# A decoder trunk on one core: head 0's gates and values take turns by two row tiles, with all first transfers on one queue in smaller parts, and one pair of heads' values a piece sooner

## The chip, the cores and the metric

The kernel runs on one core of one Trainium2 chip. The metric is the device time of one execution in microseconds (us), and the times given are medians over executions. TensorE (PE) does the matrix products, VectorE (DVE), ScalarE (ACT) and GpSimd (POOL) the elementwise work, and transfers are started from the queues of SyncE (SP), ACT and POOL.

## The reference

The input `x` is 256 rows of 2048 float32 values. Two layers are computed, each followed by a squared-ReLU MLP. The first is RetNet retention with 8 heads, the second latent attention with 16 heads. What the change touches is the projection of retention and, in one place, the attention:

```python
h = rms_norm(x, norm_mix[0])
q, k, v, gate = split(h @ w_in)         # 8 heads: q, k of 256 columns, v and gate of 512 each
q, k = apply_rope(q), apply_rope(k) * 256 ** -0.5
scores = einsum('bhcnd,bhcmd->bhcnm', q, k) * decay
o = scores @ v  (+ the state of the earlier chunk)
x = x + (silu(gate) * rms(o)) @ w_out
...
p = softmax(q_nope @ k_nope + q_pe @ k_pe, causal)      # latent attention, 16 heads
x = x + (p @ v) @ w_o
```

The norms' factors are applied late: the kernel multiplies the bare `x` (times a gain per column) by the weights, and the row factor `r0` comes in when results are read out.

## The kernel before, in words

**Numbers in two parts.** Every float32 operand of a matrix product is split into a high part (a cast on ACT, `wh` for weights) and a low part (the rest, a subtraction on DVE, `wl`), both in `split`, lines 185 to 195. One product is then three matmuls: high by high, high by low, low by high. A low part is thus first needed one matmul after its high part.

**Weights in pieces.** All weights stream through in pieces of 128 x 2048 float32 values, 1 MB, started from SP's queue into four buffers `raw`. Each piece is split in two halves of 128 x 1024 (`wh` and `wl`, five buffers each). A piece of a plain product takes 24 matmuls of 512 columns. Later heads and the MLPs use a variant (`quad`, `gemm_pair`) in which DVE also forms sums of weight blocks (lines 339 to 343) and of activations (`with_sums`, lines 419 to 421), in exchange for fewer products.

**Order by hand.** `tick` counts pieces. `later(n, fn)` puts a step into a list, to be emitted `n` pieces later. The emitted order is the order within each engine, up to a scheduler that may let an instruction pass another one on the same engine. Eight semaphores serve the transfers started from SP and ACT in turn, so that each such transfer waits until the one eight before it has landed.

**PSUM.** There are four banks `acc` for products, two banks `tp` for transposes, scores and attention outputs, and a pair `at`.

**The beginning.** For head 0, `gemm(a["ret_w_gv0"], 0, ..., "rg0", gated, start)` computes the gates in four pieces, each of four row tiles of `x` by 512 columns, into two `acc` banks. Row tiles are the 128-row tiles of the 2048 input features, 16 in all. These four pieces are loaded in parts: 256 KB twice, then 512 KB. After the first part of each half `start(half)` loads two row tiles of the transposed input (`x0t`, 256 KB) and splits them (`first_inputs`). The constants (`pos_i`, `cst`, `gpe`) are loaded at half 3. The sine tables of rope begin at half 5 (`ret_tables`; DVE casts the positions, POOL does the rest). After the gates come `rq0` and `rk0` (queries and keys, two pieces each, `gemm_t`), and then four pieces `rv0` with the values, into two `acc` banks. The loads of `x` itself share the time with `rq0` and `rk0`: `load_x`, two pieces after the last half of the gates is begun and on, brings 8 tiles of 256 KB by SP, takes their sums of squares on ACT, and writes each tile to `x_home` in DRAM from POOL's queue.

**Head 0's results.** `gated` copies the gates out of PSUM on ACT as soon as the last gate piece is done, and `silu` follows eight pieces later when `r0` is known. Rope of q and k waits six and four pieces (`ret_rope`), the scores five (`ret_scores`), the products with the values one piece after the last value piece (`ret_out`). From `ret_out` of head 0 three things are timed: the transposes and splits of its output `y`, 2 pieces later, the angles `tm` of the attention's rope on POOL, and 25 pieces later `mla_tables`, which makes the table `petab` with 16 small DVE operations (lines 575 and 578).

**Heads 1 to 7** run as `rq`, `rk` and 8 pieces `rp` each: `rp1`, `rp2`, ... In the names of the trace `rp14_wl2` would be head 1, piece 4, split 2. The trace leaves the numbers out, so they go by time here.

**Attention.** Eight pairs of heads `b` go through `query`, `turn`, `score`, a second `turn` and `values`, spaced in pieces by a table:

```python
waits = [(3, 3, 3, 2)] * 6 + [(3, 3, 2, 2), (2, 2, 2, 1)]
```

`values(b)` computes `ao` in a `tp` bank (lines 1156 and 1157), and the split of `ao` (`ot`, ACT and DVE) frees the bank. Transposes of a later pair's queries (`qntp`, `qptp`) take turns in the same two banks. After the attention comes the output product `wo`.

Of the kernel before, what the change touches and what calls it, by code (L numbers as in the profile page):

```python
# [20 lines left out]
P = 128  # L21
# [47 lines left out]
def yoco(ctx: ExitStack, tc: tile.TileContext, a):  # L69
# [141 lines left out]
                nc.tensor.transpose(tp[:, j, t * P : (t + 1) * P], srcs(t, j), ident)  # L211
        return tp

    def stream(w, chunk, cols, name, use, done=None, before=None):

        raw = pool.tile([P, 2048], F32, tag="raw", bufs=4, name=f"{name}_raw")
        if before is None:
            nc.sync.dma_start(raw[:, :cols], w[chunk])
        n = cols // 2
        for half in range(2):  # L220
            wh = pool.tile([P, 1024], F32R, tag="wh", bufs=5, name=f"{name}_wh{half}")
            wl = pool.tile([P, 1024], F32R, tag="wl", bufs=5, name=f"{name}_wl{half}")
            cuts = 1
            if before is not None:
                cuts = 1 if half else 2
                m = n // cuts
                for i in range(cuts):
                    lo = half * n + i * m
                    nc.sync.dma_start(raw[:, lo : lo + m], w[chunk][:, lo : lo + m])
                    if i == 0:  # L230
                        before(half)
# [9 lines left out]
    def piece(w, chunk, acc, act, g, nk, nb, name, before=None, done=None):  # L241

        if before is None:
            need(act, 2 * g + 2)

        def use(half, wh, wl):
            for j in range(2):
                k = g * 4 + half * 2 + j
                rh, rl = (v[:, j * nb : (j + 1) * nb] for v in (wh, wl))
                for t in range(NT):  # L250
                    ah, al = (act[k // 2][:, j, i, t * P : (t + 1) * P] for i in range(2))
                    nc.tensor.matmul(acc[t], ah, rh, start=k == 0, stop=False)
                    nc.tensor.matmul(acc[t], ah, rl, start=False, stop=False)
                    nc.tensor.matmul(acc[t], al, rh, start=False, stop=k == nk - 1)

        stream(
            w, chunk, 4 * nb, f"{name}{g}", use, done and (lambda: done(acc)),
            before and (lambda half: before(2 * g + half)),
        )

    def gemm_t(w, chunk0, act, nk, name, done):

# [163 lines left out]
    def accs(nb, name):  # L426
        return [bank("acc", [nb], f"{name}_acc{t}") for t in range(NT)]

    def gemm(w, chunk0, act, nk, nb, name, done, before=None):

        acc = accs(nb, name)
        n = nk // 4
        for g in range(n - 1):
            piece(w, chunk0 + g, acc, act, g, nk, nb, name, before)
        last_piece(w, chunk0, acc, act, nk, nb, name, done, before)

    def last_piece(w, chunk0, acc, act, nk, nb, name, done, before=None):
        g = nk // 4 - 1
        piece(w, chunk0 + g, acc, act, g, nk, nb, name, before, done)

    def gemm_blocks(w, chunk_of, act, nk, name, done):

# [73 lines left out]
    def sincos(inv, w, name, pos_f=pos_f):  # L516

        n = NT * w

        def f2k(shape, name):  # L520
            return shaped(act_tile(name, F32).rearrange("p j i s -> p (j i s)"), shape)

        ang = f2k([NT, w], f"{name}_ang")
        for t in range(NT):
            nc.gpsimd.tensor_scalar(ang[:, t], inv, pos_f[:, t : t + 1], None, op0=ALU.mult)
        flat = ang.rearrange("p t w -> p (t w)")
        k = f2k([2, n], f"{name}_k")
# [24 lines left out]
        nc.gpsimd.tensor_scalar(r, r, lim, -lim, op0=ALU.min, op1=ALU.max)  # L552

        def finish(zero):
            sc = f2k([2, n], f"{name}_sc")
            nc.scalar.activation(sc, r, AF.Sin, bias=zero)
            return sc.rearrange("p i (t w) -> p i t w", t=NT)

        return finish
# [20 lines left out]
                    )  # L580

    def ret_tables():
        nc.vector.tensor_copy(pos_f, pos_i)
        ret_sc.append(sincos(cst[:, C_INVR : C_INVR + 128], 128, "tr"))

    def scale_tables():
# [12 lines left out]
        later(2, turn)  # L599


    act0, sums0, r0, ret_sc, mla_sc, no_turn = [], [], [], [], [], []

    def first_inputs(c):

        t = f2k([2, S], f"x0t_{c}")
        nc.sync.dma_start(t, a["xt"][:, 2 * c : 2 * c + 2, :])
        v = act_tile(f"a0_{c}")
        split_act(v, t, [gain(G_MIX0 + 2 * c + j) for j in range(2)])
        act0.append(v)  # L610
# [1 line left out]
        if c in HEAD:  # L612
# [19 lines left out]
    def load_x(b):  # L632
        for t in range(NT):
            x0 = f2k([512], f"x0_{t}{b}")
            nc.sync.dma_start(x0, x_in(t, b))
            square_sum(x0, ss0[t][:, b : b + 1], f"n0_{t}{b}")
            nc.gpsimd.dma_start(x_home[t][b], x0)

    def start(half):
        first_inputs(half)  # L640
        if half == 3:
            nc.sync.dma_start(pos_i, a["pos"])
            nc.sync.dma_start(cst, a["cst"])
            nc.sync.dma_start(gpe, a["gpe"])
        if half == 5:
            ret_tables()
        if half == 7:
            for b in range(NB):
                later(2 + b, lambda b=b: load_x(b))
            later(6, scale_tables)  # L650

    def ret_rope(acc, out, name, wait):

        u = f2k([2, S], f"{name}_u")
        for i in range(2):
            nc.scalar.copy(u[:, i], acc[i][:, S:])
            nc.vector.tensor_tensor(u[:, i], acc[i][:, 0:S], u[:, i], op=ALU.add)
# [81 lines left out]

    def ret_projected(h, qk, gate, v, s):  # L740

        wait = 0 if h else 8

        def keyed(acc):
            ret_rope(acc, qk, f"rk{h}", max(wait - 4, 0))
            later(max(wait - 4, 0) + (2 if h else 1), ret_scores(h, qk, s))

        gemm_t(a["ret_w_qk"], h * 2, act0, KD, f"rq{h}", lambda acc: ret_rope(acc, qk, f"rq{h}", max(wait - 2, 0)))
# [23 lines left out]
    for h in range(RH):  # L772
        qk, gate, v, s = [], [], [], []
        if h == 0:

            def gated(acc, gate=gate):
                src = [f2k([512], f"gate_raw{t}") for t in range(NT)]
                for t in range(NT):
                    nc.scalar.copy(src[t], acc[t])

                def silu():
                    for t in range(NT):
                        g = f2k([512], f"gate0{t}")
                        nc.scalar.activation(g, src[t], AF.Silu, scale=r0[t])
                        gate.append(g)

                later(8, silu)
# [3 lines left out]
            gemm(  # L791
                a["ret_w_gv0"], 4, act0, KD, 512, "rv0",
                lambda acc, v=v, s=s, gate=gate: ret_valued(acc, 0, s, v, gate),
            )
            continue

        def paired(c, h=h, gate=gate, v=v, s=s):
# [474 lines left out]
```

## Time and profile before

| what | value |
|---|---|
| time, median of 3 runs | 2460.23 us (2459.69 to 2460.62) |
| profiled execution, its time | 2459.91 us |
| profiled execution, span from first to last instruction | 2458.1 us |
| granted TensorE clock | 1.000 |
| PE busy | 2448.9 us, 11626 matmuls |
| DVE busy | 2199.1 us |
| ACT busy | 1617.8 us |
| POOL busy | 251.1 us |
| DMA | 522.10 MB, mean 212 GB/s |

The span leaves out 1.8 us of the profiled execution's time. PE's busy time is an upper view, because matmuls overlap and their ends are modelled. The gap between the starts of two matmuls in a row tells more: it is 0.227 us for 512 columns when PE waits for nothing. A row of a timeline gives the start, the duration of one instruction or a run of them, engine, line of the kernel, operation, output and inputs, form and count. The bracket at its end gives the idle time of that engine just before it and what ended it.

### The profile page before, as it was taken

How to read it: one execution, taken by the hardware profiler on the slowest of the kernel's cores; microseconds unless marked ns; L12 is line 12 of the kernel's file. 1: busy time of each engine (PE TensorE's matmuls, PEld its weight loads, DVE VectorE, ACT ScalarE, POOL GpSimd, SP SyncE). 2: the span in 40 equal slices, each digit the busy share in tenths (PEclk: the TensorE clock that was granted, in tenths of full speed). 3: DMA queues.
4: the chain of work that ended last, by engine and by line, in shares of the span. 5: the costliest groups of instructions: out<-in, count | busy, mean ns of one | idle time of the engine just before them, and what ended most of it. 6: DMA issues, size and time to landing. Idle time of an engine off the chain costs nothing.

```text
span 2458.1 us, 31782 instructions
## 1 busy us (share of the span) xinstructions
PE 2448.9 (100%) x11626; PEld 2057.3 (84%) x11626; DVE 2199.1 (89%) x2859; ACT 1617.8 (66%) x2280; POOL 251.1 (10%) x311
## 2 busy tenths in 40 slices
PE   9999999999999999999999999999999999999999
PEld 7888888888888888888888888998888888888887
DVE  7799999889899999999999998776689999999998
ACT  6566656566676667667666777676566666676665
POOL 7400011000010010110110001100000101101101
PEclk9999999999999999999999999999999999999999
DMA  9645568546564685674785564445645856857856
GB/s 324 218 174 208 194 204 248 193 178 218 204 237 180 207 261 215 209 257 173 245 268 206 184 222 182 160 147 195 201 176 197 260 211 209 270 198 226 261 188 188
DMA packets 93980, 522.10 MB, mean 212 GB/s; under 512 B 11136, under 2 KB 12288, under 8 KB 40576
## 3 DMA queue, kind: packets, MB, share of 16 engines
q1 hardware_dynamic: 70992, 471.25, 53.4%
q0 software_dynamic: 22400, 48.25, 9.1%
q8 instruction: 91, 1.49, 0.2%
q10 hardware_dynamic: 432, 0.57, 0.1%
q14 instruction: 65, 0.53, 0.1%
HBM read 479.14 MB, written 41.94 MB: 212 GB/s over the span
## 4 chain that ended last, share of the span: by engine, by line
PE 99%; ACT 1%; DVE 0%; DMA 0%; issue 0%; POOL 0%; SPq 0%; ACTq 0%; POOLq 0%
PE u_c L378 7%; PE u_c L376 7%; PE u_c L377 7%; PE d_c L377 7%; PE d_c L378 7%; PE d_c L376 7%; PE rp_c L377 3%; PE rp_c L378 3%; PE rp_c L376 3%; PE rk_acc L280 2%; PE rq_acc L280 2%; PE u_p L376 2%; PE u_p L378 2%; PE u_p L377 2%; PE d_p L376 2%; PE d_p L377 2%
## 5 line engine op out<-in xcount | busy, mean ns | idle before, releaser
L191 ACT CAST u_wh<-u_raw 128x1024 fp32r<-128x1024 f32 x362 | 347.8, 991 | 207.5 <-DVE u_raw L339 98.3
L191 ACT CAST d_wh<-d_raw 128x1024 fp32r<-128x1024 f32 x342 | 327.4, 989 | 185.5 <-DVE d_raw L339 93.9
L192 DVE TENSOR_TENSOR u_wl<-u_raw,u_wh 128x1024 fp32r<-128x1024 f32 x362 | 401.6, 1142 | 46.2 <-ACT u_wh L191 40.9
L192 DVE TENSOR_TENSOR d_wl<-d_raw,d_wh 128x1024 fp32r<-128x1024 f32 x342 | 378.2, 1140 | 30.8 <-ACT d_wh L191 26.2
L376 PE MATMUL u_c<-u_wh,n 128*128 128x512 f32 x706 | 276.5, 392 | 0.0
L377 PE MATMUL u_c<-u_wl,n 128*128 128x512 f32 x706 | 275.6, 390 | 0.0
L378 PE MATMUL u_c<-u_wh,n 128*128 128x512 f32 x706 | 275.0, 390 | 0.0
L376 PE MATMUL d_c<-d_wh,hid 128*128 128x512 f32 x654 | 256.0, 392 | 0.0
L377 PE MATMUL d_c<-d_wl,hid 128*128 128x512 f32 x654 | 255.4, 390 | 0.0
L378 PE MATMUL d_c<-d_wh,hid 128*128 128x512 f32 x654 | 254.8, 390 | 0.0
L191 ACT CAST rp_wh<-rp_raw 128x1024 fp32r<-128x1024 f32 (+1 forms) x166 | 158.8, 981 | 128.3 <-DVE rp_raw L339 65.2
L192 DVE TENSOR_TENSOR rp_wl<-rp_raw,rp_wh 128x1024 fp32r<-128x1024 f32 (+1 forms) x166 | 183.9, 1135 | 18.5 <-ACT rp_wh L191 16.5
L378 PEld LDWEIGHTS u_c<-u_wh,n 128*128 128x128 f32 x706 | 132.5, 188 | 27.4
L376 PEld LDWEIGHTS u_c<-u_wh,n 128*128 128x128 f32 x706 | 132.6, 188 | 27.1
L377 PEld LDWEIGHTS u_c<-u_wl,n 128*128 128x128 f32 x706 | 132.6, 188 | 26.6
L378 PEld LDWEIGHTS d_c<-d_wh,hid 128*128 128x128 f32 x654 | 122.8, 188 | 25.4
L376 PEld LDWEIGHTS d_c<-d_wh,hid 128*128 128x128 f32 x654 | 122.8, 188 | 25.1
L377 PEld LDWEIGHTS d_c<-d_wl,hid 128*128 128x128 f32 x654 | 122.8, 188 | 24.6
L156 POOL DMA_DIRECT2D xh<-d_c x52 | 45.1, 867 | 934.4 <-ACT d_c L396 932.5
L191 ACT CAST ro_wh<-ro_raw 128x1024 fp32r<-128x1024 f32 x88 | 85.6, 996 | 59.4 <-DVE ro_raw L339 25.2
L376 PE MATMUL rp_c<-rp_wh,a 128*128 128x512 f32 x286 | 111.8, 391 | 0.0
L377 PE MATMUL rp_c<-rp_wl,a 128*128 128x512 f32 x286 | 111.3, 389 | 0.0
(546 smaller groups left out, 6143.6 us busy)
## 6 DMA issues: line engine op xcount, KB each, us to landing
u_raw<-in_mlp_w SPq DMA_DIRECT2D x128, 1024.0 KB, 5.3
d_raw<-in_mlp_w SPq DMA_DIRECT2D x120, 1024.0 KB, 4.9
rp_raw<-in_ret_w_gv SPq DMA_DIRECT2D x56, 1024.0 KB, 4.9
ro_raw<-in_ret_w_out SPq DMA_DIRECT2D x32, 1024.0 KB, 5.0
uq_raw<-in_mla_w_uq SPq DMA_DIRECT2D x24, 768.0 KB, 4.1
rq_raw<-in_ret_w_qk SPq DMA_DIRECT2D x16, 1024.0 KB, 4.8
rk_raw<-in_ret_w_qk SPq DMA_DIRECT2D x16, 1024.0 KB, 5.1
wo_raw<-in_mla_w_o SPq DMA_DIRECT2D x16, 1024.0 KB, 4.8
```

Source lines behind the costliest of these rows:

```text
L156: nc.gpsimd.dma_start(x_home[t][2 * p + j], part, accum_op=ALU.add)
L191: nc.scalar.copy(h, src)
L192: nc.vector.tensor_tensor(l, src, h.bitcast(F32), op=ALU.subtract)
L280: nc.tensor.matmul(acc[f], wh[:, cols], a.rearrange("p i s -> p (i s)"), start=k == 0, stop=k == nk - 1)
L376: nc.tensor.matmul(dst, ah, bh, start=n == 0, stop=False)
L377: nc.tensor.matmul(dst, ah, bl, start=False, stop=False)
L378: nc.tensor.matmul(dst, al, bh, start=False, stop=n == total[key] - 1)
```

## The change

Head 0's gate and value columns are laid side by side in DRAM by two row tiles: 8 pieces `gv0` to `gv7`, each with 12 matmuls of the gates and then 12 of the values for the same two row tiles. All four `acc` banks are held through the 8 pieces, and `rq0` and `rk0` follow them. There are 12 pieces for head 0 as before.

All first transfers are on SP's queue in smaller parts: piece 0 as four parts of 256 KB with its `x0t` as two of 128 KB, placed between them, and each other piece as 512 KB, 256 KB of `x0t`, 512 KB. `cst` is loaded in two parts. The loads of `x` move into the new loop, ahead of `gv4` to `gv7`, and the writes to `x_home` are issued from ACT's queue in place of POOL's. The cast of the positions moves from DVE to POOL, and the rope tables start at piece 2.

When the last piece is done, `raws` copies gates and values out of PSUM (four copies on ACT). Every wait of head 0 is set anew: rope 3 and 1 pieces, scores 2, `silu` 5, the values' splits 4 and `ret_out` 4 more. `ret_out` of head 0 thus comes at tick 16, where it came at 13, and with it the transposes of its `y` and `mla_tables` come three pieces later than before. The sine on ACT gets a copy in front of it that ties it behind the first rope copy (`late`). The loads of `x0s` for the sums of activations are timed anew. In the attention table the pair `b = 4` gets a last wait of 1 in place of 2.

```diff
-    def stream(w, chunk, cols, name, use, done=None, before=None):
+    def stream(w, chunk, cols, name, use, done=None, load=None):
         raw = pool.tile([P, 2048], F32, tag="raw", bufs=4, name=f"{name}_raw")
-        if before is None:
+        if load is None:
             nc.sync.dma_start(raw[:, :cols], w[chunk])
+        else:
+            load(raw)
...
-            cuts = 1
-            if before is not None:
-                cuts = 1 if half else 2
...
+            cuts = 2 if load and chunk == 0 else 1
...
+    def rows_256(acc, v, wh, wl, nb, first, last):
+        for j in range(2):
+            rh, rl = (w[:, j * nb : (j + 1) * nb] for w in (wh, wl))
+            for t in range(NT):
+                ah, al = (v[:, j, i, t * P : (t + 1) * P] for i in range(2))
+                nc.tensor.matmul(acc[t], ah, rh, start=first and j == 0, stop=False)
+                nc.tensor.matmul(acc[t], ah, rl, start=False, stop=False)
+                nc.tensor.matmul(acc[t], al, rh, start=False, stop=last and j == 1)
...
-        def finish(zero):
+        def finish(zero, late=None):
             sc = f2k([2, n], f"{name}_sc")
+            if late is not None:
+                nc.scalar.copy(sc[:, 0, 0:1], late)
             nc.scalar.activation(sc, r, AF.Sin, bias=zero)
...
     def ret_tables():
-        nc.vector.tensor_copy(pos_f, pos_i)
+        nc.gpsimd.tensor_copy(pos_f, pos_i)
...
-        sc = ret_sc[0](zero)
+        sc = ret_sc[0](zero, first_u[0][:, 0, 0:1])
...
-    def first_inputs(c):
+    def first_inputs(c, weights=None):
         t = f2k([2, S], f"x0t_{c}")
-        nc.sync.dma_start(t, a["xt"][:, 2 * c : 2 * c + 2, :])
+        if c:
+            nc.sync.dma_start(t, a["xt"][:, 2 * c : 2 * c + 2, :])
+        else:
+            for j in range(2):
+                nc.sync.dma_start(t[:, j], a["xt"][:, j, :])
+                weights(512 * j, 512 * (j + 1))
...
-            later({2: 21, 4: 14, 5: 15, 7: 17}[c], again)
+            later({2: 20, 4: 12, 5: 12, 7: 13}[c], again)
...
-            nc.gpsimd.dma_start(x_home[t][b], x0)
-
-    def start(half):
-        first_inputs(half)
-        if half == 3:
+            nc.scalar.dma_start(x_home[t][b], x0)
+
+    def start(c, raw):
+        def weights(lo, hi):
+            nc.sync.dma_start(raw[:, lo:hi], a["ret_w_gv0"][c][:, lo:hi])
+        if c == 0:
+            first_inputs(c, weights)
+            weights(1024, 1536)
+            weights(1536, 2048)
+        else:
+            weights(0, 1024)
+            first_inputs(c)
+            weights(1024, 2048)
+        if c == 1:
             nc.sync.dma_start(pos_i, a["pos"])
-            nc.sync.dma_start(cst, a["cst"])
+            nc.sync.dma_start(cst[:, :C_MASK], a["cst"][:, :C_MASK])
+        if c == 2:
+            ret_tables()
+        if c == 3:
+            nc.sync.dma_start(cst[:, C_MASK:], a["cst"][:, C_MASK:])
             nc.sync.dma_start(gpe, a["gpe"])
-        if half == 5:
-            ret_tables()
-        if half == 7:
             for b in range(NB):
-                later(2 + b, lambda b=b: load_x(b))
-            later(6, scale_tables)
+                later(1 + b, lambda b=b: load_x(b))
+            later(7, scale_tables)
...
-        wait = 0 if h else 8
         def keyed(acc):
-            ret_rope(acc, qk, f"rk{h}", max(wait - 4, 0))
-            later(max(wait - 4, 0) + (2 if h else 1), ret_scores(h, qk, s))
-        gemm_t(..., lambda acc: ret_rope(acc, qk, f"rq{h}", max(wait - 2, 0)))
+            ret_rope(acc, qk, f"rk{h}", 0 if h else 1)
+            later(2, ret_scores(h, qk, s))
+        gemm_t(..., lambda acc: ret_rope(acc, qk, f"rq{h}", 0 if h else 3))
...
-    def ret_valued(src, h, s, v, gate):
+    def ret_valued(src, h, s, v, gate, wait=1):
...
-        later(1, lambda: ret_out(h, s, v, gate, halves[h // 4]))
+        later(wait, lambda: ret_out(h, s, v, gate, halves[h // 4]))
...
-            gemm(a["ret_w_gv0"], 0, act0, KD, 512, "rg0", gated, start)
+            both = [accs(512, name) for name in ("rg0", "rv0")]
+            def raws(v=v, s=s, gate=gate):
+                src = [[f2k([512], f"{name}_raw{t}") for t in range(NT)] for name in ("gate", "v")]
+                for i in range(2):
+                    for t in range(NT):
+                        nc.scalar.copy(src[i][t], both[i][t])
...
+                later(5, silu)
+                later(4, lambda: ret_valued(src[1], 0, s, v, gate, 4))
+            for c in range(KD // 2):
+                def use(half, wh, wl, c=c):
+                    rows_256(both[half], act0[c], wh, wl, 512, c == 0, c == KD // 2 - 1)
+                stream(
+                    a["ret_w_gv0"], c, 2048, f"gv{c}", use, raws if c == KD // 2 - 1 else None,
+                    lambda raw, c=c: start(c, raw),
+                )
             ret_projected(h, qk, gate, v, s)
-            gemm(a["ret_w_gv0"], 4, act0, KD, 512, "rv0", lambda ...: ret_valued(acc, 0, s, v, gate))
...
-    waits = [(3, 3, 3, 2)] * 6 + [(3, 3, 2, 2), (2, 2, 2, 1)]
+    waits = [(3, 3, 3, 2)] * 4 + [(3, 3, 3, 1), (3, 3, 3, 2)] + [(3, 3, 2, 2), (2, 2, 2, 1)]
```

More of the change, by code (lines that the diff above doesn't have):

```diff
@@ L222, in stream @@
             wl = pool.tile([P, 1024], F32R, tag="wl", bufs=5, name=f"{name}_wl{half}")
-            cuts = 1
-            if before is not None:
-                cuts = 1 if half else 2
[L226 to L231, printed above, removed]
+            cuts = 2 if load and chunk == 0 else 1
             m = n // cuts
@@ L239, in stream, with piece @@
         tick()
-    def piece(w, chunk, acc, act, g, nk, nb, name, before=None, done=None):
-        if before is None:
-            need(act, 2 * g + 2)
-        def use(half, wh, wl):
[L247 to L259, printed above, removed]
+    def rows_256(acc, v, wh, wl, nb, first, last):
[6 more added lines that the diff above has]
+                nc.tensor.matmul(acc[t], al, rh, start=False, stop=last and j == 1)
+    def piece(w, chunk, acc, act, g, nk, nb, name, done=None):
+        need(act, 2 * g + 2)
+        def use(half, wh, wl):
+            k2 = 2 * g + half
+            rows_256(acc, act[k2], wh, wl, nb, k2 == 0, k2 == nk // 2 - 1)
+        stream(w, chunk, 4 * nb, f"{name}{g}", use, done and (lambda: done(acc)))
     def gemm_t(w, chunk0, act, nk, name, done):
@@ L427, in accs, with gemm @@
         return [bank("acc", [nb], f"{name}_acc{t}") for t in range(NT)]
-    def gemm(w, chunk0, act, nk, nb, name, done, before=None):
+    def gemm(w, chunk0, act, nk, nb, name, done):
         acc = accs(nb, name)
@@ L433, in gemm, with last_piece @@
         for g in range(n - 1):
-            piece(w, chunk0 + g, acc, act, g, nk, nb, name, before)
-        last_piece(w, chunk0, acc, act, nk, nb, name, done, before)
-    def last_piece(w, chunk0, acc, act, nk, nb, name, done, before=None):
+            piece(w, chunk0 + g, acc, act, g, nk, nb, name)
+        last_piece(w, chunk0, acc, act, nk, nb, name, done)
+    def last_piece(w, chunk0, acc, act, nk, nb, name, done):
         g = nk // 4 - 1
-        piece(w, chunk0 + g, acc, act, g, nk, nb, name, before, done)
+        piece(w, chunk0 + g, acc, act, g, nk, nb, name, done)
     def gemm_blocks(w, chunk_of, act, nk, name, done):
@@ L740, in ret_projected @@
     def ret_projected(h, qk, gate, v, s):
-        wait = 0 if h else 8
         def keyed(acc):
-            ret_rope(acc, qk, f"rk{h}", max(wait - 4, 0))
-            later(max(wait - 4, 0) + (2 if h else 1), ret_scores(h, qk, s))
-        gemm_t(a["ret_w_qk"], h * 2, act0, KD, f"rq{h}", lambda acc: ret_rope(acc, qk, f"rq{h}", max(wait - 2, 0)))
+            ret_rope(acc, qk, f"rk{h}", 0 if h else 1)
+            later(2, ret_scores(h, qk, s))
+        gemm_t(a["ret_w_qk"], h * 2, act0, KD, f"rq{h}", lambda acc: ret_rope(acc, qk, f"rq{h}", 0 if h else 3))
         gemm_t(a["ret_w_qk"], (RH + h) * 2, act0, KD, f"rk{h}", keyed)
-    def ret_valued(src, h, s, v, gate):
+    def ret_valued(src, h, s, v, gate, wait=1):
         for t in range(NT):
@@ L774, in yoco @@
         if h == 0:
[L776 to L779, printed above, removed]
+            both = [accs(512, name) for name in ("rg0", "rv0")]
[4 more added lines that the diff above has]
+                        nc.scalar.copy(src[i][t], both[i][t])
                 def silu():
@@ L783, in silu @@
                         g = f2k([512], f"gate0{t}")
-                        nc.scalar.activation(g, src[t], AF.Silu, scale=r0[t])
+                        nc.scalar.activation(g, src[0][t], AF.Silu, scale=r0[t])
                         gate.append(g)
-                later(8, silu)
-            gemm(a["ret_w_gv0"], 0, act0, KD, 512, "rg0", gated, start)
+                later(5, silu)
[7 more added lines that the diff above has]
+                )
             ret_projected(h, qk, gate, v, s)
[L791 to L794, printed above, removed]
             continue
```

5 lines of the change are left out of this document (3 added, 2 removed).

## The prediction

> **What bounds the kernel now.** I read the page's busy times first, then its chain of waits, then PE's own waits.
>
> ```profile
> PE 2448.9 (100%) x11626; PEld 2057.3 (84%) x11626; DVE 2199.1 (89%) x2859; ACT 1617.8 (66%) x2280; POOL 251.1 (10%) x311
> PE 99%; ACT 1%; DVE 0%; DMA 0%; issue 0%; POOL 0%; SPq 0%; ACTq 0%; POOLq 0%
> PE rg_acc L252 <- ACT a L194: 1.9, 2, 1.3
> PE idle L133 <- DVE zeros L130: 1.2, 1, 1.2
> PE rq_acc L276 <- DVE rq_wl L192: 1.1, 1, 1.1
> PE ao L1156 <- ACT qt L1091: 0.6, 1, 0.6
> ```
>
> PE carries 99% of the chain, and its four waits in the whole kernel are 4.8 us together. The change leaves the matmuls at their number, 11626, so it can only move waits: 1.2 us of the four (`zeros`) it does not touch, and the other three it does. No gain over some 5 us is possible, which is 0.2% of 2460 us and about what a measurement of this kernel can tell from no change. What can be lost is not so limited, so I look closely at the places where a wait can arise: the first 50 us, and the places in heads 1 and 3 and in the attention to which DVE work moves. DVE, at 89%, has little room in any of them.
>
> The beginning, on PE's timeline:
>
> ```profile
> 5.34 0.50 PE L252 MATMUL rg_acc<-rg_wh,a 128*128 128x512 f32 x1 [0.65 <-ACT a L194]
> 10.15 0.73 PE L252 MATMUL rg_acc<-rg_wh,a 128*128 128x512 f32 x2 [1.30 <-ACT a L194]
> 29.48 0.39 PE L254 MATMUL rg_acc<-rg_wh,a 128*128 128x512 f32 x1
> 29.71 0.61 PE L280 MATMUL rq_acc<-a,rq_wh 128*128 128x512 f32 x2
> 32.29 0.39 PE L280 MATMUL rq_acc<-a,rq_wh 128*128 128x512 f32 x1
> 33.81 0.39 PE L276 MATMUL rq_acc<-a,rq_wl 128*128 128x256 f32 x1 [1.13 <-DVE rq_wl L192]
> ```
>
> The step between two matmuls is 29.71 - 29.48 = 0.23 us (0.227 over longer runs). The 96 matmuls of the gates run from 5.34 to 29.71, 24.4 us where 96 x 0.227 = 21.8 would do: 2.6 us are lost, most of them before 10.15. In `rq0` the matmul after 32.29 comes 1.5 us later, 1.3 us more than a step, and with a small one behind it 1.4 us are lost there.
>
> **The change, part by part.**
>
> *The start: 1.2 us gained, and 0.1 before it.* Landings show as ACT's casts that wait for them.
>
> ```profile
> 4.01 0.62 ACT L191 CAST rg_wh<-rg_raw 128x512 fp32r<-128x512 f32 x1 [1.35 <-DMA rg_raw<-in_ret_w_gv]
> 6.01 0.62 ACT L191 CAST rg_wh<-rg_raw 128x512 fp32r<-128x512 f32 x1 [0.32 <-DMA rg_raw<-in_ret_w_gv]
> 8.64 1.04 ACT L191 CAST rg_wh<-rg_raw 128x1024 fp32r<-128x1024 f32 x1 [2.01 <-DMA rg_raw<-in_ret_w_gv]
> 6.67 0.69 DVE L192 TENSOR_TENSOR rg_wl<-rg_raw,rg_wh 128x512 fp32r<-128x512 f32 x1 [0.45 <-ACT rg_wh L191]
> 9.72 1.22 DVE L192 TENSOR_TENSOR rg_wl<-rg_raw,rg_wh 128x1024 fp32r<-128x1024 f32 x1 [2.36 <-ACT rg_wh L191]
> ```
>
> In windows (span, PE, PEld, DVE, ACT, POOL, clock, DMA share, GB/s) the transfers then go at:
>
> ```profile
> 15.00:20.00 5.00, 5.00 (x24) 4.14 (x23) 4.21 (x9) 3.91 (x7) 3.90 (x5) 1.00 0.97 295
> 10.00:30.00 20.00, 19.73 (x86) 16.05 (x87) 17.01 (x26) 13.68 (x26) 13.50 (x10) 1.00 1.02 381
> ```
>
> From 6.01 (768 KB in, `x0t` counted) to 8.64 (1280 KB in) 256 KB take 1.3 us; at 381 GB/s they take 0.7. Before, the first 12 matmuls need 768 KB, and the next 12 the 512 KB part and its whole cast (1.04) and subtraction (1.22). After, 768 KB serve 12 matmuls, and by 8.64 the values of the same two row tiles have landed as two parts, at about 7.3 and 8.6. Their casts (0.62) and subtractions (0.69) end at about 8.7 and 10.0, when PE needs the second at 10.0: 24 matmuls run through to 11.4. Then the next gates' part (1792 KB in, 8.6 + 2 x 0.7 = 10.0) has its cast (1.04) and subtraction (1.22) done at about 12.3, and PE wants the latter at 11.6: 0.7 us of wait, perhaps 0.8 with the `x0t` splits. With the second row tile's wait for its subtraction (6.67 + 0.69, 0.5, as before) the loss is 1.3 in place of 2.6. After that one piece gives PE 24 matmuls (5.4 us) per 1.25 MB where before 0.75 MB gave 2.7 us, and ACT needs 2 x 1.04 + 1.0 of those 5.4 us. I take 1.2 gained; the bounds are 0.3 (the parts' subtractions queue behind each other) and 1.6. The first matmul comes 0.1 sooner, since only 384 KB stand ahead of it, not 512.
>
> *`rq0`: 1.4 us gained.*
>
> ```profile
> 29.23 1.26 ACT L779 COPY gate_raw<-rg_acc 128x512 f32<-128x512 f32 x2 [2.02 <-PE rg_acc L254]
> 30.39 2.00 ACT L191 CAST rq_wh<-rq_raw 128x1024 fp32r<-128x1024 f32 x2
> ```
>
> Before, two copies (1.26) stand ahead of `rq0`'s second cast. After, the gates are complete 12 matmuls (2.7 us) ahead of the values, so two of the four copies run under the values' matmuls, and the other two (1.26) fall where `rq0` has its first half split already: 12 matmul pairs last 2.6 us and more from 29.71 to 32.29. I find about 0.1 us to spare, so the whole 1.4 goes; if the copies stand otherwise, up to 0.5 of it stays.
>
> *Head 1: 0.8 us lost.* The transposes of head 0's `y` come three pieces later, and their two DVE splits land in a denser place:
>
> ```profile
> 100.02 1.27 DVE L192 TENSOR_TENSOR y<-ytp,y 128x512 fp32r<-128x512 f32 x2
> 124.85 1.23 DVE L192 TENSOR_TENSOR rp_wl<-rp_raw,rp_wh 128x1024 fp32r<-128x1024 f32 x1 [0.21 <-ACT rp_wh L191]
> 131.27 4.78 DVE L192 TENSOR_TENSOR rp_wl<-rp_raw,rp_wh 128x1024 fp32r<-128x1024 f32 x4
> 132.63 0.41 PE L377 MATMUL rp_p<-rp_wl,a0s_more 128*128 128x512 f32 x1
> ```
>
> By the order of instructions on DVE they now precede a subtraction of about 121.8. From there to 132 DVE's gaps are 0.21 (124.85) and 0.26; the first subtraction of the run at 131.27 ends at 132.49, and PE uses it at 132.63, a lead of 0.14. 1.27 - 0.21 - 0.26 - 0.14 = 0.66, and as PE's low-part matmuls stand a little earlier in the new order, I take 0.8 (0 to 1.1: nothing, if the scheduler's other shifts free DVE earlier).
>
> *Head 3: 1.0 us lost.* The 16 `petab` operations of `mla_tables` move by three pieces, from a place where PE waits for nothing to just ahead of the second subtraction of `rp3`'s piece 2:
>
> ```profile
> 181.20 0.18 DVE L575 SCALAR_TENSOR_TENSOR petab<-tm_sc,gpe 128x32 f32<-128x32 f32 x1
> 182.42 0.18 DVE L575 SCALAR_TENSOR_TENSOR petab<-tm_sc,gpe 128x32 f32<-128x32 f32 x1
> 250.59 0.42 DVE L684 TENSOR_TENSOR st<-sc,dec 128x256 f32<-128x256 f32 x1 [0.47 <-PE sc L682]
> 266.48 3.64 DVE L192 TENSOR_TENSOR rp_wl<-rp_raw,rp_wh 128x1024 fp32r<-128x1024 f32 x3
> 267.76 0.50 PE L377 MATMUL rp_p<-rp_wl,a0s_more 128*128 128x512 f32 x1
> ```
>
> 12 of them take 182.42 - 181.20 = 1.22, so 16 take 1.63 us. DVE has one gap of 0.47 (250.59) and then is full to 267.70 (266.48 + 1.22), 0.06 ahead of PE's use at 267.76. 1.63 - 0.47 - 0.06 = 1.1; part of the gap is already used up by their place behind a PE result. I take 1.0 (0.3 to 1.5).
>
> *The attention, pair 4: nothing.* The first row shows the wait that the edit removes, the second why another comes:
>
> ```profile
> 1680.67 0.70 PE L1156 MATMUL ao<-pt,v 128*128 128x256 f32 x2 [0.64 <-ACT qt L1091]
> 1679.31 0.76 DVE L1030 TENSOR_TENSOR kn<-kn,kn_r 128x256 f32<-128x256 f32 x2 [0.94 <-POOL kn_r L181]
> ```
>
> One piece sooner, `ao` finds its bank free, and the 0.8 us on PE (0.64 idle and the restart) go. But its split `ot` now has to free the bank for the transposes `qptp` of the last pair. `ot`'s subtraction is queued on DVE behind `kn`, which waits for POOL and ends at 1680.07; it ends at about 1680.7, and `qptp` and the `wo` matmuls queued behind it on PE stand until then. Net 0, between 0.2 gained and 0.2 lost.
>
> *At nothing.* The position cast leaves DVE, where nothing is late at that time, for POOL, which is idle till 15 us. The eight `x_home` writes leave POOL for ACT's queue: POOL's sine chain comes sooner, and ACT issues them beside 5.4 us pieces in which it has over 2 us free. Without that room each would push a cast. The rope of q and k lies under the matmuls of the pieces that follow.
>
> Sum: 0.1 + 1.2 + 1.4 - 0.8 - 1.0 + 0 = 0.9 us gained. Against the profiled execution (2459.91, 2458.1 of span and 1.8 around it) that is 2459.0; the median of the runs lies 0.32 higher, so the forecast is **2459.3 us**.
>
> **The rivals.**
>
> *Transfers come late in `gv4` to `gv7` (slower).* The rows give KB each and median us from issue to landing.
>
> ```profile
> rg_raw<-in_ret_w_gv SPq DMA_DIRECT2D x4, 512.0 KB, 6.9
> xh<-x POOLq DMA_DIRECT2D x8, 256.0 KB, 6.6
> ```
>
> Before, gates need 4 MB and 2 MB of `x0t`, and the rest follows. After, 8.62 us to the last part's landing take 7.3 MB of weights, 1.8 of `x0t`, 2.1 of `x`, 1.6 of `x_home` writes and 0.4 of constants: 13.25 MB. At the 381 GB/s of the window from 10 to 30 this is 34.8 us, the last part lands at 43.4. The last 12 matmuls start at 5.2 + 180 x 0.227 + 1.3 = 47.4, and cast and subtraction need it 2.0 earlier, at 45.4: 2.0 us to spare. It decides below 13.25 / 36.8 = 360 GB/s. At the 295 of the window from 15 to 20 the last part lands at 53.5, 8.1 late: 2467.4 us; below 310 GB/s the kernel is slower by over 0.2%. Another form of it is the coupling of eight semaphores: parts of `gv5` and later wait for writes on ACT's queue. A write (6.6 us) and a part (6.9) behind it, with an issue on either side, would make some 15 us for two pieces that PE does in 10.9, and if that held for three pieces, PE would be 5.6 late: 2464.9. Against both: the parts are issued far ahead, four `raw` buffers deep, and 381 GB/s held over 20 us of a like mix. I give it 0.12.
>
> A rule of the Trainium skill (DMA: Bandwidth & Descriptors, "Bandwidth") speaks against the smaller parts: it wants transfers batched to 1 MB or more. The trace disagrees so far as it goes: 381 GB/s over 20 us that mix parts of 256 and 512 KB with pieces of 1 MB. The same page ("Specifications") puts a core's HBM limit at about 358 GB/s, by which, as an estimate, the last part would land at 45.6, 0.2 us late; the rows show more than that limit.
>
> *DVE keeps up (faster than forecast).* The losses of heads 1 and 3 are absorbed by slack upstream: 2460.23 - 2.7 = 2457.5. For it: a low part is used one matmul behind its high part, so the scheduler has room to turn the order, and ACT may feed DVE sooner. Against it: the leads of 0.14 and 0.06 us. 0.15.
>
> *DVE costs their upper bounds and the start brings little.* 1.1 + 1.5 lost, 0.1 + 0.3 + 0.9 gained, 0.2 in the attention: 2461.7. 0.15.
>
> *The change does not do what it says at the start:* PE waits for the first values, as it did for the second part. Gain 1.4 - 1.8 elsewhere: 2460.6. 0.06.
>
> **How the numbers follow.** The forecast holds 0.52 and spans 2457.9 to 2460.6 with its own bounds half used. The range takes in the two neighbours and their bounds, 2456.9 (all gains at their upper end, DVE free) to 2463.0 (the case of 2461.7, and late transfers of a little over a microsecond). What is left out is most of the rival on transfers and the ends of the others, under 0.2 together. Over 0.2% is 4.9 us: faster than 2455.3 would need every wait to go and no new one, 0.04; slower than 2465.2 is most of the rival on transfers (2467.4 in its first form, 2464.9 just short of it in its second), 0.10; the same 0.86.
>
> **What would show it.** In the changed kernel's trace: the first matmul at about 5.2, `gv`'s last matmul at about 50, with no wait for a transfer on ACT between 14 and 50 us that PE feels; no wait at `rq0`; a wait of some 0.5 us on a low part between 11 and 13; PE waits on `rp_wl` near 130 and near 250 to 266, under 1.5 us together each; and in the attention `qptp` waiting for DVE's `ot` in place of `ao` for ACT's `qt`. It is wrong if PE waits between 25 and 50 us, or if heads 1 to 3 lose over 3 us together.

## The result and the profile after

The changed kernel takes 2464.08 us (median of 22 runs, 2462.8 to 2466.09), the kernel before 2460.43 us in the same runs: a ratio of 1.0015, with a 95% interval of 1.0009 to 1.0021. It is 3.65 us slower, where 1 us faster was forecast, and lies 1.1 us above the stated range. The profiled execution has a span of 2461.5 us, against 2458.1.

First the page's busy times and chain, then PE's own waits:

```profile
PE 2451.7 (100%) x11626; PEld 2057.1 (84%) x11626; DVE 2198.2 (89%) x2856; ACT 1619.4 (66%) x2281; POOL 246.4 (10%) x304
PE 95%; DVE 2%; DMA 1%; ACT 1%; issue 0%; POOL 0%; SPq 0%; ACTq 0%; POOLq 0%
PE idle L133 <- DVE zeros L130: 1.2, 1, 1.2
PE qptp L211 <- DVE ot L192: 1.0, 1, 1.0
PE rp_p L371 <- DVE rp_wl L192: 0.9, 1, 0.9
PE rp_c L370 <- ACT rp_wh L191: 0.7, 1, 0.7
PE rg_acc L243 <- DVE a L195: 0.6, 1, 0.6
PE rg_acc L242 <- DVE gv_wl L192: 0.4, 1, 0.4
PE rv_acc L242 <- DVE gv_wl L192: 0.2, 1, 0.2
PE rv_acc L241 <- ACT gv_wh L191: 0.2, 1, 0.2
PE rp_p L370 <- ACT rp_wh L191: 0.2, 1, 0.2
```

The number of matmuls is the same and PE still carries nearly the whole chain, so the loss must be waits, and the list names nine where four stood. The waits of `rg_acc` for `x0t`'s split at the start and of `rq_acc` are gone in this execution, as forecast. New are two waits inside the loop of `gv` (`rg_acc`), two places in the heads (`rp_p`, `rp_c`) and `qptp`. On the timeline:

```profile
8.77 0.50 PE L241 MATMUL rv_acc<-gv_wh,a 128*128 128x512 f32 x1 [0.22 <-ACT gv_wh L191]
40.50 0.50 PE L242 MATMUL rg_acc<-gv_wl,a 128*128 128x512 f32 x1 [0.42 <-DVE gv_wl L192]
47.58 0.72 PE L243 MATMUL rg_acc<-gv_wh,a 128*128 128x512 f32 x2 [0.56 <-DVE a L195]
133.91 0.50 PE L371 MATMUL rp_p<-rp_wl,a0s_more 128*128 128x512 f32 x1 [0.93 <-DVE rp_wl L192]
270.69 0.50 PE L370 MATMUL rp_c<-rp_wh,a 128*128 128x512 f32 x1 [0.72 <-ACT rp_wh L191]
1683.79 0.44 PE L211 MATMUL qptp<-cst,qpp 128*128 128x128 f32 x2 [0.96 <-DVE ot L192]
```

An idle time in brackets leaves out the slow restart around a wait. So from here on I count a loss as the steps between the starts of PE's matmuls, less the usual step of their shape (0.227 us for 512 columns), added up over a stretch of the trace. In us, by profile (the last two are of single runs):

| stretch | before | after | writes on POOL | petab early | y later | angles in head 1 | waits back | four set | before, chain late | more bytes | before again |
|---|---|---|---|---|---|---|---|---|---|---|---|
| 0 to 20 | 2.9 | 2.0 | 2.4 | 3.0 | 3.0 | 2.5 | 2.2 | 2.3 | 3.5 | 2.4 | 4.9 |
| 20 to 60 | 1.6 | 2.0 | 0.4 | 2.7 | 2.6 | 2.3 | 2.6 | 0.6 | 0.5 | 2.1 | 1.4 |
| 126 to 145 (head 1) | 0.0 | 1.7 | 1.6 | 1.6 | 2.0 | 0.0 | 1.7 | 0.0 | 1.4 | 1.6 | 0.0 |
| 145 to 200 (head 2) | 0.8 | 0.8 | 0.7 | 0.8 | 0.9 | 2.0 | 0.7 | 0.7 | 0.7 | 0.8 | 0.7 |
| 245 to 275 (head 3) | 0.7 | 1.9 | 1.9 | 0.7 | 1.9 | 1.9 | 1.9 | 0.6 | 0.7 | 1.9 | 0.7 |
| 1600 to 1800 (attention) | 5.1 | 5.4 | 5.0 | 5.2 | 5.2 | 5.1 | 5.3 | 5.0 | 5.0 | 5.1 | 5.0 |
| whole | 21.1 | 24.1 | 22.1 | 24.8 | 26.1 | 24.9 | 24.5 | 19.4 | 21.2 | 24.2 | 22.4 |

The loss rose by 3.0 us of the spans' 3.4: -0.9 at the start, +0.4 in 20 to 60 (where the `rq0` wait went, 1.2, and the loop's two came, 1.6), +1.7 in head 1, +1.2 in head 3, +0.3 in the attention, and 0.3 in small parts elsewhere.

### The profile page after: what moved, and what is told of

Same layout as the page of the kernel before. It is cut to its first block, busy times and chain, and to the rows that moved or that the text cites. A ratio compares the mean times of both kernels' runs of the same rounds, so it can differ in the third digit from the quotient of the medians.

```text
span 2461.5 us, 31783 instructions
## 1 busy us (share of the span) xinstructions
PE 2451.7 (100%) x11626; PEld 2057.1 (84%) x11626; DVE 2198.2 (89%) x2856; ACT 1619.4 (66%) x2281; POOL 246.4 (10%) x304
## 4 chain that ended last, share of the span: by engine, by line
PE 95%; DVE 2%; DMA 1%; ACT 1%; issue 0%; POOL 0%; SPq 0%; ACTq 0%; POOLq 0%
PE u_c L372 7%; PE u_c L371 7%; PE u_c L370 7%; PE d_c L372 7%; PE d_c L371 7%; PE d_c L370 7%; PE rq_acc L274 2%; PE rp_c L370 2%; PE rp_c L371 2%; PE rp_c L372 2%; PE rk_acc L274 2%; PE u_p L371 2%; PE u_p L370 2%; PE u_p L372 2%; PE d_p L370 2%; PE d_p L371 2%
## 5 line engine op out<-in xcount | busy, mean ns | idle before, releaser
L370 PE MATMUL rp_c<-rp_wh,a 128*128 128x512 f32 x286 | 112.2, 392 | 0.7 <-ACT rp_wh L191 0.7
L372 PE MATMUL rp_c<-rp_wh,a 128*128 128x512 f32 x286 | 111.3, 389 | 0.0
```

Of the source, the lines that this page charges most:

```text
L370: nc.tensor.matmul(dst, ah, bh, start=n == 0, stop=False)
L372: nc.tensor.matmul(dst, al, bh, start=False, stop=n == total[key] - 1)
```

## The experiments

Their medians are of 10 or 11 runs, and of two experiments there is one run each. The intervals are some 0.2% wide, so a single experiment's time can barely tell a microsecond. The verdicts rest on the place of the waits in the traces, and the times stand beside them.

**x_home written from POOL again.**

```diff
-            nc.scalar.dma_start(x_home[t][b], x0)
+            nc.gpsimd.dma_start(x_home[t][b], x0)
```

> The changed kernel with one line back: the eight writes to x_home are issued from POOL's queue again, not ACT's, so that they leave the turn of eight semaphores that SP's and ACT's transfers share. Theory A (coupling): PE's waits at 39.7 and 46.6 us (0.6 and 0.7 us, with restarts 1.6 us) come because SP's queue waits for a write's semaphore; they go, the queue has no 3 us gap near 27 us, and the time falls by 1.2 to 1.6 us. Theory B (bandwidth): the same bytes pass in the same time, the two waits stay within 0.3 us and the time stays.

Measured: 2462.41 us (ratio to before 1.0009, 1.0 to 1.0018), 1.7 below the changed kernel. Both waits in the loop are gone; 20 to 60 us loses 0.4. In the changed kernel SP's queue waits for writes are these (engine and line, releaser, us in total, times, longest), with two of its rows on the timeline and two windows (span, PE, PEld, DVE, ACT, POOL, clock, DMA share, GB/s):

```profile
SPq L645 <- DMA xh<-x: 6.1, 2, 3.5
SPq L637 <- DMA xh<-x: 3.5, 2, 2.9
26.93 0.33 SPq L645 DMA_DIRECT2D gv_raw<-in_ret_w_gv  x1
30.16 0.80 SPq L637 DMA_DIRECT2D x<-in_x  x2
30.00:35.00 5.00, 5.00 (x24) 4.14 (x23) 4.28 (x4) 3.19 (x7) 4.70 (x4) 1.00 0.92 255
10.00:50.00 40.00, 39.02 (x169) 30.94 (x169) 29.74 (x31) 26.88 (x46) 34.96 (x25) 1.00 1.01 371
```

SP stands 9.6 us for landings of writes (it stands for landings of loads too, in both kernels). Between 26.93 and 30.16 it issues nothing, and the window behind that moves 255 GB/s, where the whole loop has 371. With the writes on POOL's queue the same window moves more:

```profile
30.00:35.00 5.00, 5.00 (x24) 4.14 (x23) 3.54 (x4) 3.89 (x9) 4.84 (x4) 1.00 1.04 407
```

The pause alone is not the harm. With the writes on POOL's queue SP also issues nothing from 26.49 to 29.29 us, but then seven loads are still under way. In the changed kernel, just before 30.16, two loads and two writes are. So the writes' turn of semaphores holds SP's queue and leaves it few loads ahead. But on POOL's queue, behind its other work, six of the eight writes also start at 43 us or later, so 1.6 MB left the loop too. Whether that is the cause was tried next.

**The same with more bytes.** A kernel like the one above, with four loads added:

```diff
+            if b < 2:
+                extra = act_tile(f"extra_{t}{b}", F32)
+                nc.sync.dma_start(extra...[:, 0:512], a["ret_w_gv0"][b][:, t * 512 : (t + 1) * 512])
```

> The kernel of the first experiment (changed, x_home written from POOL's queue) with four more loads of 256 KB on SP's queue, beside the first four loads of x; what they bring is not used. They put 1.05 MB more ahead of the weights of gv4 to gv7, as much as the four writes that POOL's queue issues later than ACT's did. Theory A (coupling to the writes' landing): SP's queue has no wait for a write, the weights land about 2.6 us later than in the first experiment (gv7's last part at about 44 for 41.5), still ahead of their use, and PE loses under 0.5 us between 20 and 50 us. Theory B (bytes): PE loses 1.5 us or more there, as in the changed kernel.

Four writes is also what the traces give for the time that counts. When the last part of `gv7` landed, six writes had landed in the changed kernel, with a seventh under way, and two in the first experiment. Measured in one run: 2463.02 us. SP waits for no write, and `gv6` and `gv7` don't wait on PE: the last part lands at 44.2, as expected. But PE loses 0.8 us at `gv5`, right behind the added bytes, and 1.1 in `rq0`, whose first piece is pushed back:

```profile
35.45 0.74 PE L242 MATMUL rg_acc<-gv_wl,a 128*128 128x512 f32 x2 [0.23 <-DVE gv_wl L192]
53.20 0.50 PE L270 MATMUL rq_acc<-a,rq_wl 128*128 128x256 f32 x2 [0.84 <-DVE rq_wl L192]
```

Neither theory's number holds (under 0.5, or 1.5 and more, before 50 us). The waits at 40 and 47 need SP's standing for the writes; yet the stretch has so little to spare that a megabyte more costs as much, elsewhere. The landing of `gv7`'s last part shows both shares: 41.5 us in the first experiment, 44.2 here, 46.3 in the changed kernel. So some 2.6 us of the delay come with the bytes (up to 0.7 more for the seventh write, an estimate from 256 KB at the 397 GB/s of 10 to 50 us in the first experiment), and the rest with the standing. The rates agree: from 10 to 50 us the changed kernel moves 371 GB/s, the first experiment 397, and this one 395. How PE's 1.6 us divide between the two stays open.

**petab early.**

```diff
-            later(25, mla_tables)
+            later(22, mla_tables)
```

> The changed kernel with mla_tables 22 pieces after ret_out of head 0 in place of 25, which by the order of instructions puts the 16 petab operations back from about 249 us (head 3) to about 182 us (head 2), and moves nothing else of note. Theory A (those operations are the loss of head 3): the waits on rp_wh and the loss of 1.25 us between 250 and 271 us go, 1.0 to 1.3 us. Theory B (head 3 is late because of what heads 1 and 2 passed on): they stay.

Measured: 2463.12 us (1.0011, 1.0002 to 1.002). Head 3's loss falls from 1.9 to 0.7, what it was before, and its wait on `rp_wh` is gone. Theory A holds: the 16 operations are all of it.

**y later.**

```diff
-        later(2, turn)
+        later(2 if h else 7, turn)
```

> The changed kernel with the transposes of head 0's y seven pieces after ret_out in place of two, so that its two DVE splits (1.28 us) leave the dense stretch from 113 to 133 us. Theory A (the splits are the loss of head 1): the wait on rp_wl near 133 us falls from 1.2 + 0.4 us by 1.3. Theory B (POOL's chain of angles beside DVE is the loss): it falls by little, under 0.5. Both: by about 1.3 with DVE's operations still 0.08 us longer each than before the change.

Measured: 2464.94 us (1.002, 1.0011 to 1.0029). Head 1's loss does not fall, it is 2.0. The splits of `y`, which my forecast held for the cause, are not it.

**The angles in head 1.**

```diff
-        if h == 0:
+        if h == 1:
             no_move, pos = small(1, "no_move"), small(NT, "pos_m")
...
-            later(25, mla_tables)
+            later(15, mla_tables)
```

> The changed kernel with POOL's chain of angles for the attention's rope (20 us of POOL operations) started by head 1's ret_out in place of head 0's, so that POOL is idle between 106 and 128 us; the petab operations keep their place near 249 us. Theory A (only the order on DVE counts): the loss of 1.64 us near 133 us stays. Theory B (DVE operations are lengthened while POOL runs beside them): DVE's operations from 115 to 128 us return to their usual length (1.21 for 1.32, 0.55 for 0.81, 0.68 for 0.77), and the loss falls by 0.8 to 1.2 us, to the 0.8 that was forecast or less; a part may come back near 165 to 185 us.

Measured: 2464.75 us (1.0016, 1.0008 to 1.0025). Head 1's loss is gone (1.7 to 0.0), more than expected, with the splits of `y` still there; 1.2 of it comes back in head 2, where the chain now runs. The DVE rows of the same four operations in a row and of the later run of subtractions, first in the changed kernel with one POOL row beside them, then here:

```profile
115.16 1.32 DVE L333 TENSOR_TENSOR rp_raw<-rp_raw 128x1024 f32<-128x1024 f32 x1
116.40 0.81 DVE L192 TENSOR_TENSOR sl<-st,sh 128x384 fp32r<-128x384 f32 x1
117.14 0.84 DVE L413 TENSOR_TENSOR a0s_sum<-x0s 128x256 f32<-128x256 f32 x2
117.90 0.75 DVE L414 TENSOR_TENSOR a0s_sum<-a0s_sum,x0s 128x128 f32<-128x128 f32 x2
132.63 4.77 DVE L192 TENSOR_TENSOR rp_wl<-rp_raw,rp_wh 128x1024 fp32r<-128x1024 f32 x4
115.72 1.07 POOL L535 TENSOR_TENSOR tm_rr<-tm_rr,tm_part 128x128 f32<-128x128 f32 x1
```

```profile
116.08 1.21 DVE L333 TENSOR_TENSOR rp_raw<-rp_raw 128x1024 f32<-128x1024 f32 x1
117.22 0.55 DVE L192 TENSOR_TENSOR sl<-st,sh 128x384 fp32r<-128x384 f32 x1
117.69 0.75 DVE L413 TENSOR_TENSOR a0s_sum<-x0s 128x256 f32<-128x256 f32 x2
118.36 0.48 DVE L414 TENSOR_TENSOR a0s_sum<-a0s_sum,x0s 128x128 f32<-128x128 f32 x2
131.96 5.91 DVE L192 TENSOR_TENSOR rp_wl<-rp_raw,rp_wh 128x1024 fp32r<-128x1024 f32 x5
```

From the `rp_raw` sum to the run of subtractions that PE waits for, the changed kernel takes 132.63 - 115.16 = 17.47 us and this one 131.96 - 116.08 = 15.88: 1.6 us more for the same DVE work, which is the loss.

**The kernel before, with the chain late.**

```diff
+            hold = act_tile("hold", F32).rearrange("p j i s -> p (j i s)")
+            nc.gpsimd.tensor_scalar(hold[:, 0:1], no_move, 0.0, None, op0=ALU.mult)
+            for _ in range(12):
+                nc.gpsimd.memset(hold, 0.0)
+            nc.gpsimd.tensor_scalar(no_move, hold[:, 0:1], 0.0, None, op0=ALU.mult)
```

> The kernel before with one thing added: twelve memsets on POOL (nothing of them is used) between head 0's factor and POOL's chain of angles, which holds the chain back by some 13 us, to where the changed kernel has it (106 to 128 us). The transposes of y, the petab operations and all transfers stay. Theory A (the chain beside a dense DVE stretch is all of head 1's loss): PE loses 1.4 to 1.7 us near 132 us, and the time rises by as much. Theory B (it needs the moved y splits as well): under 0.8 us.

Measured: 2461.51 us against 2459.47 of the kernel before beside it (1.0008, 0.9999 to 1.0018). Head 1 loses 1.4 us, where it lost nothing, by the same wait:

```profile
PE rp_p L377 <- DVE rp_wl L192: 0.9, 1, 0.9
92.77 12.09 POOL L718 MEMSET hold<- 128x1024 f32 x12
95.33 0.75 DVE L665 TENSOR_TENSOR rq_v<-rq_u,rope_tab 128x256 f32<-128x256 f32 x2
96.68 2.35 DVE L192 TENSOR_TENSOR rp_wl<-rp_raw,rp_wh 128x1024 fp32r<-128x1024 f32 x2
```

Moving POOL's chain is enough for 1.4 of the 1.7 us. (The time's interval still takes in no change; the wait is what shows it.) The rows give a second reading. In the kernel before, the chain itself ran there, and the same operations took longer than beside the memsets:

```profile
95.91 0.88 DVE L665 TENSOR_TENSOR rq_v<-rq_u,rope_tab 128x256 f32<-128x256 f32 x2
97.48 2.61 DVE L192 TENSOR_TENSOR rp_wl<-rp_raw,rp_wh 128x1024 fp32r<-128x1024 f32 x2
```

0.88 for 0.75 and 2.61 for 2.35: it is not that POOL is busy that lengthens DVE's work, but what POOL does. Beside the memsets the operations take 0.42 and 1.22 us each, as they do where POOL idles. The Trainium skill (SBUF — State Buffer, "Who interferes with whom") says that a DVE instruction with two inputs in SBUF contends with a GpSimd instruction that reads SBUF, and not with one that only writes it. The trace agrees: the operations above read two SBUF tiles and are lengthened by the chain (reads and writes) and not by memsets (writes alone).

**The attention's wait back.**

```diff
-    waits = [(3, 3, 3, 2)] * 4 + [(3, 3, 3, 1), (3, 3, 3, 2)] + [(3, 3, 2, 2), (2, 2, 2, 1)]
+    waits = [(3, 3, 3, 2)] * 6 + [(3, 3, 2, 2), (2, 2, 2, 1)]
```

> The changed kernel with the attention's table of waits as before (pair 4 with 2 in place of 1). Theory A (one wait for another, as forecast): the wait of qptp for DVE's ot (1.0 us, 1.1 with the restart) goes, the wait of ao for ACT's qt (0.64, 1.0 with the restart) comes back, and the time moves by 0.1 to 0.3 us, less than the runs can tell. Theory B (the edit is a gain or a loss of its own): one of the two waits is gone without the other.

Measured: 2464.41 us (1.0017, 1.0009 to 1.0026). `qptp` no longer waits for `ot`, and `ao` waits for `qt` again:

```profile
PE ao L1179 <- ACT qt L1114: 0.8, 1, 0.8
```

The loss in the attention is 5.3 with the old table and 5.4 with the new (5.0 to 5.2 in the other profiles, whichever table they have). One wait stands for the other.

**Four things set otherwise together.** Writes on POOL, the attention's old waits (the diff is as above), `mla_tables` after 22 pieces, and the chain started behind `no_turn`:

```diff
-            nc.scalar.dma_start(x_home[t][b], x0)
+            nc.gpsimd.dma_start(x_home[t][b], x0)
...
         no_turn.append(zero)
+        pos = small(NT, "pos_m")
+        nc.gpsimd.tensor_scalar(pos, pos_f, zero, None, op0=ALU.add)
+        mla_sc.append(sincos(cst[:, C_INVM : C_INVM + 32], 32, "tm", pos))
...
         if h == 0:
-            ...
-            later(25, mla_tables)
+            later(22, mla_tables)
```

> The changed kernel with four things set otherwise: x_home written from POOL's queue, the attention's waits as before, mla_tables 22 pieces after ret_out, and POOL's chain of angles started right behind no_turn (about 60 us), where DVE has two subtractions for each 5.5 us. If the losses found so far are separate and add, the loop's waits (1.6 us), head 1's loss (1.64) and head 3's (1.25) all go, with no new one near 180: 2464.1 - 4.5 - 0.2 = 2459.4 us, 1 us below the kernel before. If POOL's chain costs wherever it runs, 1 us or so of it shows between 60 and 90 us; if they do not add, the time stays above 2460.4.

Measured: 2459.72 us against 2460.08 of the kernel before beside it (0.9998, 0.9989 to 1.0007). It is 4.4 below the changed kernel's median where 4.7 was expected (4.0, if each is taken against the kernel before beside it), and PE's waits are down to four, `zeros` and these:

```profile
PE rv_acc L241 <- ACT gv_wh L191: 0.7, 1, 0.7
PE ao L1177 <- ACT qt L1112: 0.7, 1, 0.7
PE rv_acc L242 <- DVE gv_wl L192: 0.2, 1, 0.2
```

The losses are separate and add, and the chain costs little from 62 to 82 us, where DVE has room: from 60 to 90 us PE loses 1.1 us, against 0.9 in the changed kernel. DVE is busy there for 22.5 of 30 us, where from 113 to 133 us of the changed kernel it is busy for 19.4 of 20. The trace loses 1.7 us less than before's; the runs can't tell this version from the kernel before.

**The kernel before once more.**

> The kernel before, profiled once more, to see how much of the first 20 us is chance: its loss there was 2.9 us in the one profile, the changed kernel's 2.0 to 3.0 us in five. If before's lies at 2.9 again, the gain of the start is about 0.3 us on average; if it lies within 2.0 to 2.6, there is none.

Measured in one run: 2461.98 us, and a loss of 4.9 us in the first 20, not 2.9. With the 3.5 of the chain kernel, whose start is the same, before's start loses 2.9 to 4.9 and the changed one 2.0 to 3.0 in eight profiles. There is a gain, 0.9 us between the two profiled executions and 1.3 between the means (3.8 and 2.5), and its size is chance in good part. The first two rows of the table together say what became of it. Over the first 60 us the kernel before loses 4.0 to 6.3 us in three profiles and the changed one 4.0 to 5.7 in the five with writes on ACT's queue. With the writes on POOL's it loses 2.8 and 2.9 (4.5 with the added bytes). What the new beginning gains, the loop's waits take back.

## Why the prediction was wrong

**At nothing.** This is the first step that failed. The prediction costed the move of the writes to ACT's queue at nothing, with ACT's free time as the cover, and named the coupling of the semaphores as the second form of its first rival, at some 5.6 us. (Its own terms give another figure: 15 us against 10.9 for two pieces is 6.2 us for three, and 4.2 after the 2.0 us to spare.) The mechanism of the rival came, with two pieces late and 1.6 us, and with it the sign that the prediction had named for being wrong, PE waits between 25 and 50 us. The last part of `gv7` landed at 46.3 us, where 43.4 was forecast and 45.4 was needed. The bandwidth form did not come as it was put: the stretch from 10 to 50 us moved 371 GB/s, above the 360 that it needed, and still two pieces were late, with SP's queue standing in between. The bytes have a share, though: without the standing, a megabyte more put that landing back by 2.6 us.

**Head 1: right place, wrong cause, half the size.** 0.8 was forecast and 1.7 came. Two things were wrong and one hid the other. The splits of `y` cost nothing (moving them away left the loss at 2.0). Eight transposes on PE move with them, as the timeline of the kernel with the angles in head 1 shows:

```profile
114.44 0.60 PE L211 MATMUL ytp<-cst,y 128*128 128x128 f32 x4
116.27 0.61 PE L211 MATMUL ytp<-cst,y 128*128 128x128 f32 x4
```

They take PE about as long as the splits take DVE: counted from the scores of head 1, PE's first use of the late subtraction stands at 20.2 us where before it stood at 19.2, and the lead of 0.15 us is kept. The transposes were left out of the step. And the prediction listed the chain of angles on POOL nowhere as a cost, though it moves from 93 to 115 us to 106 to 128 us, beside a stretch in which DVE has hardly a gap.

**Head 3: right, by another wait.** 1.0 forecast, 1.2 measured, gone when the 16 operations go back. The wait was forecast on the low part `rp_wl` and came on the high part `rp_wh`: DVE's late sum `rp_raw` holds ACT's cast, and the cast holds PE at 270.69.

```profile
269.59 3.91 ACT L191 CAST rp_wh<-rp_raw 128x1024 fp32r<-128x1024 f32 x4 [0.40 <-DVE rp_raw L337]
```

In the emitted order the 16 operations move by three pieces, on the chip by 67 us (182 to 249). They read ACT's sine `tm_sc`, which moves from 177.8 to 247.3 us; why it moves so far is not shown.

**The start: right in direction, its size open.** 1.3 was forecast; 0.9 came between the two profiles and 1.3 between the means, by luck as much as by reckoning, for one of its terms was off. The first values' part was put at 7.3, half way to the landing of the 512 KB part, but its cast runs at 8.10:

```profile
8.10 0.62 ACT L191 CAST gv_wh<-gv_raw 128x512 fp32r<-128x512 f32 x1 [1.79 <-DMA gv_raw<-in_ret_w_gv]
```

The second part landed at 9.08, where 8.6 was forecast. So half a transfer did not land at half the time here; why is not shown. In the other profiles with this start the first values' part landed between 7.8 and 9.0.

**`rq0`: right in direction, its size open too. The attention: right.** 1.2 us of the 1.4 went between the two profiled executions. But in the two other profiles with before's start only 1.0 and 0.3 us were lost there, and with `petab` early 0.8 in the changed order. The attention's two waits changed places for nothing.

With the forecast's own terms set to what was measured (0.9 + 1.2 - 1.7 - 1.2) the sum is a loss of 0.8 us, and the loop's 1.6, the attention's 0.3 (no more than profiles of one table differ by) and small parts of 0.3 bring it to 3.0. At 0.15% the result lies within 0.2% of before, the likeliest of the three cases, on its slow side. The range's upper end took the heads at 2.6 lost, the attention at 0.2, the gains at 1.3 and late transfers at 1.3, a loss of 2.8 in all. The trace has 2.9, 0.3, 2.1, 1.6 and the small parts, 3.0 in all. So 0.2 of the 1.1 us beyond the range are in these terms, and another 0.2 in the kernel before, whose median is 2460.43 in these runs. The other 0.7 lie between the traces' 3.0 and the medians' 3.65 and stay open. Chance in the beginning is of that size: the four other profiles with its transfers lose 0.8 to 1.7 us more in the first 60 us than the profiled execution.

## What to carry to other kernels

Where a step is moved, follow every engine that it uses: PE transposes that moved along went with the DVE work at no loss here, and a POOL chain that moved along cost 1.4 to 1.7 us. Before moving writes to another queue, ask which semaphores they share with the loads, because here a load whose turn came after a write stood, with all that was queued behind it, until the write had landed. Where leads are 0.06 and 0.15 us, little is absorbed: in head 1 1.6 us of longer DVE work cost PE 1.7 us, in head 3 1.6 us of moved operations cost 1.2.

## What the runs showed that was not expected

POOL instructions that read SBUF lengthen DVE instructions with two SBUF inputs: 0.81 for 0.55, 1.32 for 1.21, while twelve memsets of 1.0 us each beside the same kind of work left it at its usual length. A DVE instruction with one of its two inputs in PSUM, the scores' product `st` at 114.62 us, took 0.42 us beside the chain and 0.42 without it.

In the second profile of the kernel before, PE idled 0.8 and 1.7 us around its first 12 matmuls, and the granted clock then fell to half for some 3 us (a window, with the clock third from the end):

```profile
12.00:14.00 2.00, 2.00 (x6) 1.61 (x5) 2.00 (x5) 1.70 (x4) 0.00 (x0) 0.50 1.05 385
```

The steps rose from 0.227 to 0.43 us and about 1.5 us were lost. The other profiles had waits of up to 1.65 us there at the full clock, so whether the waits brought the lower clock is not shown.
